# A trunk kernel on one core: the last block's sum and logits move into the first routing, its norm behind its own routing

## Chip, cores and metric

The kernel runs on one core of a Trainium2 chip. The metric is the device time of one execution in microseconds (us). Engines are named as in the profile: PE (products), PEld (PE's weight loads, which overlap them), DVE (vector), ACT (scalar), POOL (GpSimd), SP (which here only issues DMAs).

## What is computed

One layer over 16 learned meta tokens and 512 tokens of width 1024: an input norm, a mixer (stick-breaking attention and an RWKV-7 time mix with gates, then `w_out`), a residual norm, a mixture of experts, a last norm. The last half matters here:

```python
h = layer_norm(ALPHA * h + mix, ln1_g[l], ln1_b[l])
ff = moe_ffn(h, router_w, router_b, wg, wu, wd)
h = layer_norm(ALPHA * h + ff, ln2_g[l], ln2_b[l])
...
logits = (t @ router_w) + router_b          # 16 experts in 4 groups of 4
probs = softmax(logits)
group_score = sum(top_k(grouped, 2)[0])     # best group by its two best experts
gate = top_val / sum(top_val)               # the two best experts of that group
out = sum over experts e of combine[:, e] * ((silu(t @ wg[e]) * (t @ wu[e])) @ wd[e])
```

## The kernel before, in words

The tokens lie in four blocks of 128 (blocks 0 to 3; tiles `hb[0]` to `hb[3]`, printed as hb_5422 to hb_5425). The mixer's end, the routing and the experts follow each other, with every engine's instructions in the order in which the program records them (`in_order`, called after the experts, binds each engine to that order).

*w_out and the residual norm.* For each block b the products of `w_out` (L1319) fill two halves of 512 columns. `half_in(b, n, pt)` adds a half to the scaled residual (L1457) and takes its statistics (L1460); `stats(b)` joins them (L1464, L1466) and has POOL raise the variance to the power -0.5 (L1467). `turn(b, q)` transposes four 128-column pieces on PE (L1475), ACT copies them out (L109, tile h1T). `logits(b, q)` multiplies four pieces with the router's weights (L1484, 16 columns wide); with q = 1 DVE scales the result (L1486, tile lg). `store_h1(b, n)` norms `hb[b]` in place on DVE (L1494 and L1495; for block 3 in two halves) and SP stores it (L1496) into h1_d, from which the experts' tokens are gathered later. The products for block b carry the transposes and logits of block b-1 between them.

*Routing.* `route(lo, hi)` is a generator for blocks lo to hi-1. Its first part (L1385 to L1392, with one ACT exponential) ranks the experts within their groups; then it makes the masks of the chosen experts and expert pairs (L1393 to L1408, tiles msk). Up to the first `yield` all this is one piece. The second piece counts positions: PE products of the pair masks with triangular or full ones (L1413, 24 columns wide), read by DVE (L1415, tile posx). `early = route(0, 3)` does blocks 0 to 2, `late = route(3, 4)` block 3.

*One-hots and picks.* `one_hot_f` turns positions into one-hots (L1514, tile ohf). `pick(b)` multiplies block b with its one-hots (L1509): 8 products of 128 columns, each with two weight loads in the trace, so 16 rows of PEld. Their sums over the four blocks are the tokens of the first tile of expert work, copied out by ACT to the tile x. pick(b) reads `hb[b]` after the norm. The last pick, `pick(3)`, stands outside the shown function, before `gates()`, which computes the gate values on DVE and POOL (L1434 to L1449, tile info).

*Fillers.* `warm(n)` issues n products of the identity with itself (L430), whose result nobody reads. Here 8 stand before the positions of block 3 and 12 behind its one-hot.

*Experts.* 12 tiles of 128 places (4 slots of 32), 6 passes of 16 products each per tile (L1720 for gate and up, L1731 for down), 72 passes in all. 96 weight blocks of 1 MB are fetched by SP (L1293) in the order of use into 18 buffers. A pass that was the last to use a buffer frees it for the next fetch. Between the passes stand the products that make token indices and gates from the one-hots (L1594), POOL's gathers of tokens by index from h1_d (L1623), their transposes (L1639), and the last norm with the scattered store (L1629).

The order around the change is that of the recorded calls:

```python
    logits(3, 0)
    next(early)
    turn(3, 1)
    one_hot_f(0, 3)
    store_h1(3, 1)
    pick(0)
    logits(3, 1)
    late = route(3, 4)
    next(late)
    pick(1)
    pick(2)
    warm(WARM_R[0])
    next(late)
    one_hot_f(3, 4)
    warm(WARM_R[1])
```

Of the kernel before, what the change touches and what calls it, by code (L numbers as in the profile page):

```python
# [44 lines left out]
SOLVE_RATE = 1.0  # L45
SY = (5.0, 1.4, 1.4)
WARM = 16
WARM_R = (8, 12)
HSD = 4
OVT = 6  # L50
LY = 6
# [17 lines left out]
def trunk(ctx, tc, A, out):  # L69
# [29 lines left out]
    def sm():  # L99
        return bank("sm")  # L100
# [7 lines left out]
    def act(out, in_, func, **kw):  # L108
        ins = nc.scalar.activation(out, in_, func, **kw)  # L109
        if func in (AF.Exp, AF.Ln, AF.Sigmoid, AF.Tanh, AF.Silu) and not tc.in_control_flow:  # L110
            if tables["load"] is not None:
                order(ins, tables["load"])
            tables["users"].append(ins)
        return ins
# [310 lines left out]
    def warm(n):  # L425

        if n:
            pw = sm()
            for _ in range(n):
                nc.tensor.matmul(pw[:, 0:128], ident, ident, start=True, stop=True)  # L430
# [931 lines left out]
    def route(lo, hi):  # L1362
# [27 lines left out]
        act(e, e, AF.Exp)  # L1390
        V.tensor_tensor(gt, gt, eq, op=OP.add)
        V.tensor_reduce(rv, gt, axis=AX.X, op=OP.add)  # L1392
        V.scalar_tensor_tensor(tp, rank, 2.0, e, op0=OP.is_lt, op1=OP.mult)  # L1393
        V.tensor_scalar(two, rank, 2.0, None, op0=OP.is_lt)
        V.tensor_reduce(g1.rearrange("p n g -> p (n g)"), tv, axis=AX.X, op=OP.add)
# [74 lines left out]
    def turn(b, q):  # L1470
        if not q:
            TT[b, "T"] = P4.tile([128, KD, 128], FT, name="h1T", bufs=2)
        pt = sm()
        for k in range(4):
            nc.tensor.transpose(pt[:, k * 128:(k + 1) * 128], hb[b][:, (4 * q + k) * 128:(4 * q + k + 1) * 128], ident)  # L1475
        act(TT[b, "T"][:, 4 * q:4 * q + 4], pt.rearrange("p (k t) -> p k t", k=4), AF.Copy)

    def logits(b, q):

        if not q:  # L1480
            TT[b, "l"] = sm()
        pl = TT[b, "l"]
        for k in range(4 * q, 4 * q + 4):
            nc.tensor.matmul(pl[:, 0:NE], TT[b, "T"][:, k, :], rwg[:, k, :], start=k == 0, stop=k == KD - 1)  # L1484
        if q:
            nc.vector.scalar_tensor_tensor(lg[:, b], pl[:, 0:NE], TT[b, "n"][0], rb2, op0=OP.mult, op1=OP.add)  # L1486

    def store_h1(b, n):

        rs, mean = TT[b, "n"]  # L1490
        for h in range(0, 2, n):
            cs = slice(512 * h, 512 * h + 512 * n)
            z = hb[b][:, cs]
            nc.vector.scalar_tensor_tensor(z, z, mean, g1r[:, cs], op0=OP.subtract, op1=OP.mult)  # L1494
            nc.vector.scalar_tensor_tensor(z, z, rs, b1r[:, cs], op0=OP.mult, op1=OP.add)  # L1495
            nc.sync.dma_start(h1_d[128 * b:128 * b + 128, cs], z)  # L1496
# [7 lines left out]
    def pick(b, hs=(1, 0)):  # L1504


        for h in hs:
            for k in range(4):
                nc.tensor.matmul(PX[h][:, k], hb[b][:, 512 * h + 128 * k:512 * h + 128 * k + 128], OHF[:, b],  # L1509
                                 start=b == 0 and k == 0, stop=b == 3 and k == 3)  # L1510

    def one_hot_f(lo, hi):

        nc.vector.tensor_tensor(OHF[:, lo:hi].rearrange("p n (q s) -> p n q s", q=4),  # L1514
                                iota_1[:, None, None, 0:CAP].to_broadcast([128, hi - lo, 4, CAP]),
                                posx[:, lo:hi, 0:4, None].to_broadcast([128, hi - lo, 4, CAP]), op=OP.is_equal)
# [7 lines left out]
    for b in range(4):  # L1524
        pt = acc() if b else PZ[4]
        for k in range(0 if b else 4, 8):
            if k == 2 and b:
                turn(b - 1, 1)
                store_h1(b - 1, 2)
            if k == 3 and b:  # L1530
                logits(b - 1, 0)
            if k == 4 and b:
                logits(b - 1, 1)
            if k == 6:
                turn(b, 0)
            w_out(pt, b, WO[2 + k // 4], k)
            if k == 4 and b == 3:
                PX = [acc().rearrange("p (k t) -> p k t", k=4) for _ in range(2)]
                for u in PX:
                    nc.vector.memset(u, 0.0)  # L1540
                early = route(0, 3)
                next(early)
        half_in(b, 1, pt)
        stats(b)
    logits(3, 0)
    next(early)
    turn(3, 1)
    one_hot_f(0, 3)
    store_h1(3, 1)
    pick(0)  # L1550
    logits(3, 1)
    late = route(3, 4)
    next(late)
    pick(1)
    pick(2)
    warm(WARM_R[0])
    next(late)
    one_hot_f(3, 4)
    warm(WARM_R[1])
    p4.__exit__(None, None, None)  # L1560
    hp_pool.__exit__(None, None, None)

# [381 lines left out]
```

## Time and profile before

| | |
|---|---|
| median of 3 runs | 875.85 us (873.61 to 877.27) |
| the profiled execution | 873.92 us |
| its span, first to last instruction | 872.2 us |
| mean granted TensorE clock | 0.959 |
| PE / PEld busy | 804.0 us (92%) / 522.4 us (60%) |
| DVE / ACT / POOL busy | 422.0 / 317.2 / 294.2 us |
| HBM traffic | 195 GB/s over the span |

The span is what the profiler saw between the first and the last instruction; the execution's time has 1.7 us around it. Times in the rows below count from the start of the span. A row of the timeline gives start, duration, engine, line, operation and tiles (out<-in); a bracket tells how long the engine was idle before it and what ended that. The granted clock (PEclk) is the share of full speed: 1.00 is 2.4 GHz, 0.50 is 1.2 GHz.

### The profile page before, as it was taken

What the parts mean: (1) busy time and instruction counts of PE and PEld (TensorE: products, weight loads), DVE (VectorE), ACT (ScalarE), POOL (GpSimd) and SP (SyncE); (2) the same over time, 40 slices, a digit from 0 to 9 for tenths busy, and PEclk for the clock granted to TensorE, in tenths of its full rate; (3) what the DMA queues carried; (4) which work ended last, traced back from release to release, by engine and by line L of the source; (5) the groups of instructions that cost most, each with busy time, mean ns of one, the idle gap of its engine ahead of it and who ended that gap; (6) DMA issues with size and microseconds to landing.
All of it is one profiled execution on the core that took longest, in us unless ns stands there. A gap on an engine that the chain in (4) does not pass through costs nothing. (4 is left out here: it accounts for less than half of the span.)

```text
span 872.2 us, 16061 instructions
## 1 busy us (share of the span) xinstructions
PE 804.0 (92%) x6476; PEld 522.4 (60%) x6476; DVE 422.0 (48%) x795; ACT 317.2 (36%) x639; POOL 294.2 (34%) x339
## 2 busy tenths in 40 slices
PE   6989999989898989969998999899999999999993
PEld 5877777867888867747666877773333333333331
DVE  7565664741476669981554788720123112202214
ACT  6466564655756575525555332111010010010000
POOL 3266766651433444955552001120101200300102
PEclk8999898999999999988998999889999999999996
DMA  4521111136432225433315979599799999999800
GB/s 149 183 60 49 49 49 50 49 101 222 137 105 86 84 75 157 145 98 98 93 56 174 311 247 390 206 353 325 258 383 387 375 385 387 377 386 386 303 1 27
DMA packets 127234, 169.17 MB, mean 194 GB/s; under 512 B 7106, under 2 KB 62476, under 8 KB 127156
## 3 DMA queue, kind: packets, MB, share of 16 engines
q1 hardware_dynamic: 122228, 158.00, 52.8%
q10 hardware_dynamic: 2944, 5.90, 1.9%
q0 software_dynamic: 1984, 4.21, 1.4%
q8 instruction: 52, 0.85, 0.4%
q14 instruction: 26, 0.21, 0.1%
HBM read 152.29 MB, written 17.89 MB: 195 GB/s over the span
## 5 line engine op out<-in xcount | busy, mean ns | idle before, releaser
L237 POOL TENSOR_TENSOR w_lo<-w_raw,w_hi 128x512 fp32r<-128x512 f32 x87 | 123.4, 1421 | 169.1 <-ACT w_hi L109 151.2
L1720 PE MATMUL bank<-raw,x 128*32 128x512 f32 x1536 | 170.9, 594 | 1.9 <-ACT hid L109 1.2
L335 PE MATMUL bank<-hT_hi,w_hi 128*128 128x264 f32 (+1 forms) x512 | 149.1, 347 | 3.4 <-ACT w_hi L109 1.6
L335 PE MATMUL bank<-hT_hi,w_lo 128*128 128x264 f32 (+1 forms) x512 | 138.6, 327 | 8.0 <-POOL w_lo L237 8.0
L335 PE MATMUL bank<-hT_lo,w_hi 128*128 128x264 f32 (+1 forms) x512 | 137.2, 324 | 0.0
L1720 PEld LDWEIGHTS bank<-raw,x 128*32 128x32 f32 x1536 | 47.9, 110 | 104.8 <-issue 102.3
L335 PEld LDWEIGHTS bank<-hT_hi,w_hi 128*128 128x128 f32 x512 | 87.1, 193 | 18.3 <-ACT w_hi L109 2.7
L335 PEld LDWEIGHTS bank<-hT_hi,w_lo 128*128 128x128 f32 x512 | 86.8, 193 | 16.5 <-POOL w_lo L237 11.6
L335 PEld LDWEIGHTS bank<-hT_lo,w_hi 128*128 128x128 f32 x512 | 86.5, 192 | 7.2
L1731 PE MATMUL bank<-raw,h 128*32 128x512 f32 x768 | 87.0, 594 | 0.0
L1694 POOL TENSOR_TENSOR ln_f<-ln_f,mhalf 128x1 f32<-128x1 f32 x12 | 11.5, 956 | 184.6 <-DVE ln_f L1693 184.6
L109 ACT ACTIVATE w_hi<-w_raw 128x512 fp32r<-128x512 f32 x100 | 62.3, 624 | 24.6 <-DMA w_raw<-in_w_in_dram 9.0
L1649 DVE SCALAR_TENSOR_TENSOR hid<-hid,gat,bank 128x512 f32<-128x512 f32 x12 | 9.0, 747 | 120.9 <-PE bank L1720 64.5
L1731 PEld LDWEIGHTS bank<-raw,h 128*32 128x32 f32 x768 | 23.4, 110 | 50.8 <-issue 50.8
L568 POOL TENSOR_TENSOR R<-zs,R 128x144 f32<-128x144 f32 (+3 forms) x32 | 44.8, 1421 | 18.6 <-DVE R L566 18.6
L1319 PE MATMUL bank<-raw,hT_hi 128*128 128x512 f32 x128 | 44.6, 404 | 0.4 <-ACT hT_hi L109 0.4
L109 ACT ACTIVATE h<-bank 128x512 f32<-128x512 f32 x12 | 7.2, 597 | 97.5 <-PE bank L1639 97.5
L109 ACT ACTIVATE x<-bank 128x512 f32<-128x512 f32 x14 | 8.4, 597 | 83.2 <-PE bank L1639 74.3
L109 ACT ACTIVATE hid<-bank 128x512 f32<-128x512 f32 x12 | 7.1, 595 | 72.3 <-PE bank L1720 72.3
L1467 POOL TENSOR_TENSOR ln_rs<-ln_ve,mhalf 128x1 f32<-128x1 f32 x4 | 5.3, 1328 | 79.2 <-DVE ln_ve L1466 79.2
L566 DVE TENSOR_TENSOR_SCAN R<-ones_r,ab 128x144 f32<-128x144 f32 (+3 forms) x32 | 31.9, 1036 | 0.0
L556 DVE COPY zs<-bank 128x264 f32<-128x264 f32 (+3 forms) x40 | 15.3, 432 | 33.9 <-ACT ab L109 33.8
(349 smaller groups left out, 1334.5 us busy)
## 6 DMA issues: line engine op xcount, KB each, us to landing
raw<-in_exp_w_gate_dram SPq DMA_DIRECT2D x32, 1024.0 KB
raw<-in_exp_w_up_dram SPq DMA_DIRECT2D x32, 1024.0 KB
raw<-in_exp_w_down_dram SPq DMA_DIRECT2D x32, 1024.0 KB
w_raw<-in_w_in_dram SPq DMA_DIRECT2D x84, 256.0 KB
raw<-in_w_out_dram SPq DMA_DIRECT2D x4, 1024.0 KB
sig_d<-sg ACTq DMA_DIRECT2D x8, 264.0 KB
sig<-sig_d SPq DMA_DIRECT2D x8, 264.0 KB
xin<-in_x_dram SPq DMA_DIRECT2D x4, 512.0 KB
```

What stands on the lines that cost most here:

```text
L109: ins = nc.scalar.activation(out, in_, func, **kw)
L237: eng.tensor_tensor(lo[:, ks], raw[:, ks], hi[:, ks].bitcast(FT), op=OP.subtract)
L335: nc.tensor.matmul(pt[:, :e - s], w_[:, k % 4, :], m[:, k, s:e], start=(k == 0 and n == 0), stop=(k == KD - 1 and n == 2))
L556: nc.vector.tensor_copy(zs[:, h, s:e], pz[h][:, :e - s])
L566: nc.vector.tensor_tensor_scan(R[:, h, :W][:, ::-1], ones_r[:, :W], ab[:, h, :W][:, ::-1], 0.0, op0=OP.mult, op1=OP.add)
L568: nc.gpsimd.tensor_tensor(R[:, h, :W], z[:, h], R[:, h, :W], op=OP.subtract)
L1319: nc.tensor.matmul(pt, MG[x][:, k, 128 * b:128 * b + 128], w[y][:, k % 4, :], start=(k == 0 and i == 0), stop=(k == 7 and i == 2))
L1467: nc.gpsimd.tensor_tensor(rs, ve, mhalf, op=OP.pow)
L1649: nc.vector.scalar_tensor_tensor(hid, hid, gate, pu, op0=OP.mult, op1=OP.mult)
L1694: nc.gpsimd.tensor_tensor(rs, ve, mhalf, op=OP.pow)
L1720: nc.tensor.matmul(P[k[0]][32 * i:32 * i + 32], x_of(t, i, kk), W[k, e][0][:, s], start=kk == 0, stop=kk == 7)
L1731: nc.tensor.matmul(Y[g, p // 2][r:r + 32], H[t][:, s, 32 * i:32 * i + 32], W[unit_of(k, i), e][0][:, s], start=s == 0 and not second, stop ...
```

## The change

The routing's generator gets one more `yield`, between the ranks and the masks. The last block's sum (`half_in(3, 1)` and `stats(3)`) is recorded after the ranks of blocks 0 to 2 and before their masks. The second half of its logits goes ahead of the positions of blocks 0 to 2 and of all picks; its ranks and masks are taken directly behind the first one-hots; its norm and store go behind its own one-hot, in front of pick(2) and pick(3). Of twenty fillers four are left, ahead of pick(0).

```diff
-WARM_R = (8, 12)
+WARM_R = 4
...
         V.tensor_tensor(gt, gt, eq, op=OP.add)
         V.tensor_reduce(rv, gt, axis=AX.X, op=OP.add)
+        yield
         V.scalar_tensor_tensor(tp, rank, 2.0, e, op0=OP.is_lt, op1=OP.mult)
...
     logits(3, 0)
     next(early)
     turn(3, 1)
+    logits(3, 1)
+    next(early)
     one_hot_f(0, 3)
-    store_h1(3, 1)
-    pick(0)
-    logits(3, 1)
+    warm(WARM_R)
     late = route(3, 4)
     next(late)
+    next(late)
+    pick(0)
     pick(1)
-    pick(2)
-    warm(WARM_R[0])
     next(late)
     one_hot_f(3, 4)
-    warm(WARM_R[1])
+    store_h1(3, 1)
+    pick(2)
```

The lines of the changed kernel are one higher from the new `yield` on (L1415 becomes L1416) and two higher behind this stretch (L1594 becomes L1596). How the instructions stand on the two engines concerned:

PE before, from the end of the positions of blocks 0 to 2 (tile msk_2213) to the first expert products (raw: weights):

```order
L1413 MATMUL bank<-msk_2213,tri 128x24
L1475 MATMUL bank<-ident,hb_5425 128x128 x4
L1509 MATMUL bank<-ohf,hb_5422 128x128 x8
L1484 MATMUL bank<-rwg,h1T 128x16 x4
L1509 MATMUL bank<-ohf,hb_5423 128x128 x8
L1509 MATMUL bank<-ohf,hb_5424 128x128 x8
L430 MATMUL bank<-ident 128x128 x8
L1413 LDWEIGHTS ones_b
...
L430 MATMUL bank<-ident 128x128 x12
L1509 MATMUL bank<-ohf,hb_5425 128x128 x8
L1720 MATMUL bank<-raw,x 32x512 x16
```

PE now, from the first half of block 3's logits on:

```order
L1485 MATMUL bank<-rwg,h1T 128x16 x4
L1476 MATMUL bank<-ident,hb_5425 128x128 x4
L1485 MATMUL bank<-rwg,h1T 128x16 x4
L1414 LDWEIGHTS tri
...
L430 MATMUL bank<-ident 128x128 x4
L1510 MATMUL bank<-ohf,hb_5422 128x128 x8
L1510 MATMUL bank<-ohf,hb_5423 128x128 x8
L1414 LDWEIGHTS ones_b
...
L1510 MATMUL bank<-ohf,hb_5424 128x128 x8
L1510 MATMUL bank<-ohf,hb_5425 128x128 x8
L1722 MATMUL bank<-raw,x 32x512 x16
```

The transposes and the second logits of block 3 went ahead of the first positions; the positions of block 3 went ahead of pick(2); between picks 0 and 1 nothing is left, and pick(3) follows pick(2) directly.

DVE now, from the ranks of blocks 0 to 2 to the ranks of block 3 (before, the four rows from hb_5425 to ln_ve stood behind the pair masks, and the scaled logits lg behind the norm of block 3):

```order
L1392 TENSOR_REDUCE r_rank<-r_gt 128x48
L1458 SCALAR_TENSOR_TENSOR hb_5425<-hb_5425,bank 128x512
L1461 BN_STATS l_st<-hb_5425 128x6
L1465 BN_AGGR ln_mv<-l_st 128x2
L1467 TENSOR_SCALAR ln_ve<-ln_mv 128x1
L1394 SCALAR_TENSOR_TENSOR r_tp<-r_rank,r_e 128x48
...
L1409 TENSOR_TENSOR msk_2213<-msk_2212 128x24
L1487 SCALAR_TENSOR_TENSOR lg<-bank,ln_rs,rb_2219 128x16
L1416 SCALAR_TENSOR_TENSOR posx<-bank,msk_2213 128x72
L1515 TENSOR_TENSOR ohf<-iota_2191,posx 128x384
L1385 TENSOR_TENSOR r_eq<-lg 128x64
```

And DVE now, behind the positions of block 3 (before, r_ky of the gates came directly behind the one-hot):

```order
L1416 SCALAR_TENSOR_TENSOR posx<-bank,msk_2213 128x24
L1515 TENSOR_TENSOR ohf<-iota_2191,posx 128x128
L1495 SCALAR_TENSOR_TENSOR hb_5425<-hb_5425,ln_mv,g1r 128x512
L1496 SCALAR_TENSOR_TENSOR hb_5425<-hb_5425,ln_rs,b1r 128x512
L1495 SCALAR_TENSOR_TENSOR hb_5425<-hb_5425,ln_mv,g1r 128x512
L1496 SCALAR_TENSOR_TENSOR hb_5425<-hb_5425,ln_rs,b1r 128x512
L1435 TENSOR_TENSOR r_ky<-e_2200,msk_2212 128x64
```

The four norm steps of block 3 stand between its one-hot and the gates. ACT and POOL keep their order; on SP the read of the overflow flag (tile xc_i) goes from the middle of the expert loads to behind the last one, and the two stores of block 3 keep their place ahead of the loads that follow them.

## Rows read from the trace of the kernel before

**Rows 1.** Table of stretches: busy (count) of PE, PEld, DVE, ACT, POOL; PEclk, DMA share, GB/s.

```profile
600.00:860.00 260.00, 256.97 (x2416) 83.15 (x2408) 52.44 (x130) 19.27 (x33) 31.59 (x29) 1.00 0.87 316
820.00:840.00 20.00, 20.00 (x188) 6.17 (x184) 0.75 (x1) 1.19 (x2) 0.00 (x0) 1.00 0.20 75
```

**Rows 2.** Timeline, PE and PEld, from w_out's end to the experts.

```profile
557.99 0.40 PE L1319 MATMUL bank<-raw,hT_hi 128*128 128x512 f32 x1
...
558.29 1.06 PE L1484 MATMUL bank<-rwg,h1T 128*128 128x16 f32 x8
...
560.59 0.19 PE L1413 MATMUL bank<-msk,tri 128*128 128x24 bf16 x1 [1.24 <-DVE msk L1408]
...
561.17 0.66 PE L1475 MATMUL bank<-ident,hb 128*128 128x128 f32 x4 [0.27 <-DVE hb L1457]
...
563.06 3.49 PEld L1509 LDWEIGHTS bank<-ohf,hb 128*128 128x128 f32 x16 [1.47 <-DVE ohf L1514]
...
566.42 1.83 PEld L1484 LDWEIGHTS bank<-rwg,h1T 128*128 128x128 f32 x8
...
573.57 1.87 PEld L430 LDWEIGHTS bank<-ident 128*128 128x128 f32 x16
...
575.36 0.24 PEld L1413 LDWEIGHTS <-ones_b 128*128 128x128 bf16 x3
...
578.22 1.87 PEld L1509 LDWEIGHTS bank<-ohf,hb 128*128 128x128 f32 x16
...
580.97 3.64 PE L1720 MATMUL bank<-raw,x 128*32 128x512 f32 x32 [0.69 <-ACT x L109]
```

**Rows 3.** Table of stretches, as rows 1: the picks.

```profile
562.00:572.00 10.00, 8.94 (x42) 8.94 (x43) 6.50 (x25) 1.96 (x3) 2.71 (x6) 0.50 0.57 194
572.00:581.00 9.00, 8.31 (x80) 8.11 (x80) 2.42 (x10) 1.20 (x2) 2.21 (x7) 1.00 1.05 390
```

**Rows 4.** Timeline, DVE, the same stretch.

```profile
558.25 0.21 DVE L1393 SCALAR_TENSOR_TENSOR r_tp<-r_rank,r_e 128x48 f32<-128x48 f32 x1
...
560.43 0.68 DVE L1457 SCALAR_TENSOR_TENSOR hb<-hb,bank 128x512 f32<-128x512 f32 x1
...
562.19 0.22 DVE L1415 SCALAR_TENSOR_TENSOR posx<-bank,msk 128x72 f32<-128x72 f32 x1
562.45 0.56 DVE L1514 TENSOR_TENSOR ohf<-iota,posx 128x384 f32<-128x384 f32 x1
562.92 0.74 DVE L1494 SCALAR_TENSOR_TENSOR hb<-hb,ln_mv,g1r 128x512 f32<-128x512 f32 x1
...
565.26 0.75 DVE L1495 SCALAR_TENSOR_TENSOR hb<-hb,ln_rs,b1r 128x512 f32<-128x512 f32 x1
...
568.67 0.23 DVE L1385 TENSOR_TENSOR r_eq<-lg 128x64 f32<-128x64 f32 x1
...
571.29 0.17 DVE L1408 TENSOR_TENSOR msk<-msk 128x8 bf16<-128x8 bf16 x1
575.76 0.18 DVE L1415 SCALAR_TENSOR_TENSOR posx<-bank,msk 128x24 f32<-128x24 f32 x1 [4.31 <-PE bank L1413]
...
576.19 0.22 DVE L1434 TENSOR_TENSOR r_ky<-e,msk 128x64 f32<-128x64 f32 x1
```

**Rows 5.** Timeline, ACT: the copy behind block 3's last transposes.

```profile
561.86 0.60 ACT L109 ACTIVATE h1T<-bank 128x512 f32<-128x512 f32 x1 [3.62 <-PE bank L1475]
```

**Rows 6.** Timeline, SP's queue: the first expert load behind the stores.

```profile
566.46 0.39 SPq L1293 DMA_DIRECT2D raw<-in_exp_w_up_dram  x1
```

**Rows 7.** Timeline, POOL and PEld: gates' end, first gather, its first use.

```profile
579.97 0.21 POOL L1449 TENSOR_TENSOR info<-r_ab,info 128x8 bf16<-128x8 f32 x1
586.44 1.20 POOL L1623 DMA_INDIRECT hb<-h_d,idx  x1 [6.26 <-DMA g2h<-in_ln_g_dram]
...
592.73 0.42 PEld L1639 LDWEIGHTS bank<-ident,hb 128*128 128x128 f32 x4 [0.84 <-DMA hb<-h_d,idx]
```

**Rows 8.** Table of stretches, as rows 1: an earlier slow stretch.

```profile
384.00:398.00 14.00, 10.24 (x158) 7.54 (x160) 6.29 (x6) 4.73 (x8) 6.90 (x7) 0.51 0.25 75
```

## The prediction

> **What bounds the kernel now.** Start at the end. The table of stretches for 600 to 860 us shows PE busy 256.97 of 260 us at a clock of 1.00 [rows 1]: the expert stage is one unbroken row of products, so whatever moves its first product (L1720) moves the end by as much. The table also shows the cover of that claim: the DMA engines are busy only 0.20 of 820 to 840 us, some 4 us of full traffic, so the last weights are in near 824, while products go on to about 857 (260 less 257 us is 3 us of idle time at the end) [rows 1]. Next, the timeline says what the first expert product waits for. It starts at 580.97, released by ACT's copy of the gathered tokens, which is released by the last product of `pick(3)` [rows 2]. So read PE backwards from there: pick(3) 578.22, the position products of block 3 (L1413) at 575.36, fillers (L430) from 573.57, picks 1 and 2 before them, the second half of the logits of block 3 from 566.42 for 1.83, pick(0) from 563.06 [rows 2]. The clock of this stretch is 0.50 from 562 to 572 and 1.00 after it [rows 3]. That is 1.2 and 2.4 GHz, and the same 16 weight loads take 3.36 us (563.06 to 566.42) at the one and 1.79 us (573.57 to 575.36) at the other [rows 2].
>
> On DVE the masks of block 3 are done at 571.29 + 0.17 = 571.46 [rows 4], yet their products start at 575.36: they stand behind picks 1 and 2 and eight fillers. The twelve further fillers then hold pick(3) until 578.22, though its one-hot is finished by about 576.2, when the next DVE operation (r_ky) begins [rows 2, 4].
>
> **The change, step by step.** I call X the moment when the position products of block 3 start on PE (575.36 before; the expert stage follows 580.97 - 575.36 = 5.61 later).
>
> *Sum of block 3 ahead.* Its four DVE steps now follow the rank instead of the masks. They can start when the last w_out product ends, 557.99 + 0.40 = 558.4 [rows 2]. From the sum to the operation behind the variance took 562.19 - 560.43 = 1.76 [rows 4], so the second half of the first routing starts at 560.2 instead of 558.25. From it to the mask products took 560.59 - 558.25 = 2.34 [rows 2, 4], so those come at 562.6, 2.0 later than before. This is the cost of the move.
>
> *Logits of block 3 early.* The transposes came 561.17 - 560.43 = 0.74 behind the start of the sum [rows 2, 4]: now 559.2, directly behind the first half of the logits (558.29 + 1.06 = 559.35). The copy starts 0.69 behind them and takes 0.60 [rows 5], so the second half of the logits runs from 560.5 to 561.6, in a hole in which PE only waits for masks. It leaves the middle of the picks, where it took 1.83 us at half clock [rows 2]. POOL's power for the scale is issued at the same distance behind the variance as before and is wanted two microseconds later: free.
>
> *First pick.* The positions are read 0.40 behind the start of their products (575.36 to 575.76), the one-hot follows 0.26 later (562.19 to 562.45) and pick(0) 0.61 after that (562.45 to 563.06) [rows 2, 4]: 562.6 + 0.4 + 0.26 + 0.61 = 563.8. The four fillers in front are eight loads: 0.9 us at full and 1.7 us at half rate behind mask products that end near 562.75, so 563.7 or 564.5. I take 564.5, 1.4 later than before.
>
> *Masks of block 3.* They begin 0.47 behind the start of the one-hot (562.45 to 562.92), at 563.7, and take 571.29 - 568.67 = 2.62 [rows 4]: ready near 566.5, long before PE gets to them. So X is now set by PE alone: pick(0) and pick(1), 32 loads, no logits and no fillers between.
>
> *How long that takes is the unknown*, since it is the clock's. Lower end: 32 loads at 1.79 / 16 = 0.112 is 3.6 us, from 563.8: X = 567.4. Upper end: all at 3.36 / 16 = 0.21 is 6.8 us, from 564.5: X = 571.3. Before, PE waited 1.24 us for the masks, 0.27 for the sum and 1.47 for the one-hot among narrow products, and the clock fell [rows 2, 3]. The changed order still has a wait of some 0.7 us for the copy and 1.0 us for the masks among products 16 and 24 columns wide, so I expect the fall again, after these waits. It came back about 9 us after pick(0) began, with the narrow logits in between; behind these, picks alone ran for 572 - 568.2 = 3.8 us until it rose. Without the logits I take some 4 us of half rate from 564.5: 4.1 / 0.213 = 19 loads, the other 13 at 0.112 in 1.5 us, X = 570.1.
>
> *Norm of block 3 behind its routing.* It now stands between the one-hot and pick(3), which reads the normed block. From X: positions 0.40, then one-hot and next operation 0.43 (575.76 to 576.19), then four norm steps that took 565.26 + 0.75 - 562.92 = 3.09 [rows 4], the left half done after some 1.5 of them. The left half is ready at X + 2.4, the right at X + 3.9. On PE, pick(2) covers X + 0.2 to X + 2.0, half of pick(3) X + 2.4 to X + 3.3, the other half X + 3.9 to X + 4.8. The copy and its release took 580.97 - 578.22 - 1.79 = 0.96 behind the last load [rows 2]. The experts start at X + 5.75: PE waits about 1.0 us for DVE here, which it did not before.
>
> *Result of the chain.* X = 570.1 gives 575.8, 5.2 us before 580.97; the ends 567.4 and 571.3 give 573.1 (7.8 earlier) and 577.0 (3.9 earlier).
>
> *What moves behind it.* SP: the two stores of block 3 stood ahead of seven expert loads, the first issued at 566.46 [rows 6]; the stores now wait for the norm (X + 3.9 = 574.0), so the loads go about 8 us later. Cover: the program first wants one of them in the eighth pass of products, 7 passes of about 3.6 us (the first is 3.64 [rows 2]) or 25 us after the start. Lag and earlier start together are 8 + 5.2 = 13 us, less than the 33 us from the last weights to the last product, even if half of those are the last passes' own; if that cover were gone, what exceeds it would come back as a stall. SP's read of the overflow flag moves behind its last load and holds nothing. DVE and POOL: the gates start at X + 3.9; from r_ky to the end of POOL's last step took 579.97 + 0.21 - 576.19 = 4.0 [rows 4, 7], so they are done at X + 7.9, and are wanted after the first pass, X + 5.75 + 3.6 = X + 9.3. Spare 1.4 us, was 4.4. POOL: the first token gather is issued at 586.44, 5.5 us behind the first product, and used by the transposes at 592.73 [rows 7]; this shifts as a whole, but the delayed loads now stand in the DMA queues beside it. Bounds 0 and 2.7 us (one more block of 1 MB at the 390 GB/s of 572 to 581 [rows 3]); I take 0.2, near the lower, since the engines were already full then (share 1.05).
>
> Sum: 5.2 - 0.2 = 5.0 us. The profiled execution took 873.92 us, 872.2 of it span; so 868.9 for one like it. It lies 1.9 below the median of 875.85; against the median, 870.8.
>
> **The clock rule.** The trace shows the clock down for 10 us in a stretch where PE was busy 8.94 of 10.00 us [rows 3]. The Trainium skill ("TensorE: Matmul & The Clock Gate", Part 1, "What's actually happening") says that "the default state is throttled, and activity releases the throttle". It speaks against taking away sixteen of the twenty fillers, whose only output is activity; by it alone the low clock could last through all picks, which is the third rival below. The trace agrees so far that a stretch of narrow products does not keep the clock up.
>
> **Rivals.** 0.5% of 875.85 is 4.4 us, about what a measurement here can tell from no change.
>
> 1. *The clock never falls*, or only for a moment: X = 567.4, 7.8 - 0.2 = 7.6 us, 868.2. For it: the waits among the narrow products shrink from 1.24 + 0.27 + 1.47 us to about 1.9 us, with fillers before pick(0). Against: what PE does between them is still narrow. Chance 0.12.
> 2. *Low through both first picks, or a late gather*: X = 571.3, 3.9 less 0 to 2.7; about 872.4. Chance 0.20.
> 3. *Low to the last pick*: 48 loads at 0.213 = 10.2 us and 0.2 from 564.5 end at 574.9, pick(3) at 578.3, experts at 579.3: 1.7 earlier, 874.2. For it: the fillers are gone and PE now waits for the norm as well; from 384 to 398 us the clock was 0.51 with PE busy 10.24 of 14.00 us [rows 8]. Against: unbroken picks brought it back in 3.8 us. Chance 0.13.
> 4. *Low into the experts, slower than before.* If the waits for the norm keep or bring the low clock at the first expert products, each pass of 3.6 us becomes about 7.2 at half rate. After rival 3 (1.7 gained) one such pass loses 1.9 net, and from the second on it shows: 7.2 - 1.7 = 5.5 us, 881.4. Against: the waits are 0.4 and 0.6 us within 3 us of full-width products, and the 0.69 us wait before the experts left the clock at 1.00 [rows 2, 3]. Chance 0.05.
>
> That the change doesn't do what it says is partly so already: pick(2) is meant to cover the norm and covers half of it; that is in the sum.
>
> **How the numbers follow.** The forecast (X between 569.5 and 571.0, 869.9 to 871.8) has chance 0.50 and is the likeliest: 870.8. Its upper edge crosses 4.4 us of gain: I count 0.46 of it as faster. Faster: 0.46 + 0.12 = 0.58. Same: 0.04 + 0.20 + 0.13 = 0.37. Slower: 0.05. The range takes in the forecast, rival 1 (868.2) and rival 2 with half of the gather's bound, 0.82 together, and half a microsecond of scatter at the ends: 867.6 to 873.6.
>
> **What would show it.** In the changed profile: transposes of block 3 near 559.2 and the logits ahead of the mask products near 562.6; pick(0) between 563.7 and 564.6; X near 570 with nothing between the picks before it; PE waiting about 0.4 and 0.6 us for hb from L1496 inside pick(3); experts 5.75 behind X and from there 291 us to the end. It is wrong if the clock is 0.50 at the first expert pass, if PE waits for DVE or POOL at L1596, for the gather at L1641, or for a weight.

## Result and the profile after

The changed kernel takes 870.09 us in the median of six runs (869.74 to 872.0). The kernel before, run beside it, took 877.74 us (873.61 to 879.67). The ratio on record is 0.9935 with a 95% interval of 0.9906 to 0.9964 (it is not the quotient of these two medians, which is 0.9913). So it is faster, as forecast, though the upper end of the interval falls short of the 0.5% that the prediction counted as faster. The forecast was 870.8, in a range of 867.6 to 873.6. One run in this document, of the kernel before without fillers (882.11 us), was in a slower state and is left out of its median and ratio. The profiled execution took 870.13 us with a span of 868.4, against 873.92 and 872.2 before.

Spans of two profiles can't be subtracted as they are. The last `w_out` product starts at 557.99 before [rows 2] and at 559.76 now, and in the twelve other profiles of this study at 557.93 to 565.15, although nothing that PE does ahead of it was edited. So I count from that start, written with a plus sign: experts at +22.98 means 22.98 us behind it.

Timeline of PE in the changed kernel, from that product to the first use of gathered tokens (columns as in [rows 2]; L1485 logits, L1414 positions, L430 fillers, L1510 picks, L1722 experts):

```profile
559.76 0.40 PE L1319 MATMUL bank<-raw,hT_hi 128*128 128x512 f32 x1
...
562.29 1.06 PE L1485 MATMUL bank<-rwg,h1T 128*128 128x16 f32 x8 [0.69 <-ACT h1T L109]
564.46 0.18 PE L1414 MATMUL bank<-msk,tri 128*128 128x24 bf16 x1 [1.10 <-DVE msk L1409]
...
564.62 2.05 PE L430 MATMUL bank<-ident 128*128 128x128 f32 x8
566.46 4.34 PE L1510 MATMUL bank<-ohf,hb 128*128 128x128 f32 x32
570.63 0.23 PE L1414 MATMUL bank<-msk,ones_b 128*128 128x24 bf16 x3
...
572.95 1.16 PE L1510 MATMUL bank<-ohf,hb 128*128 128x128 f32 x8 [0.18 <-DVE hb L1496]
574.40 1.16 PE L1510 MATMUL bank<-ohf,hb 128*128 128x128 f32 x8 [0.29 <-DVE hb L1496]
576.24 3.64 PE L1722 MATMUL bank<-raw,x 128*32 128x512 f32 x32 [0.69 <-ACT x L109]
...
589.25 0.66 PE L1641 MATMUL bank<-ident,hb 128*128 128x128 f32 x4 [1.17 <-DMA hb<-h_d,idx]
```

The positions of block 3 now stand directly behind picks 0 and 1. The experts start at +16.48 (576.24 - 559.76) instead of +22.98, which is 6.50 earlier. Two new waits follow the edit: pick(3) waits twice for the norm (hb, L1496), and the transposes of the first gathered tokens wait 1.17 us for a DMA.

The stretches of the same profile (columns as in [rows 1]):

```profile
560.00:570.00 10.00, 8.21 (x62) 7.84 (x62) 7.22 (x36) 2.10 (x4) 2.13 (x6) 0.83 0.01 2
564.30:567.71 3.41, 3.25 (x20) 3.25 (x20) 2.85 (x17) 1.46 (x2) 0.00 (x0) 0.50 0.02 5
...
581.70:589.20 7.50, 6.38 (x76) 1.90 (x68) 0.17 (x1) 0.00 (x0) 3.22 (x3) 1.00 1.05 334
...
600.00:855.00 255.00, 252.98 (x2386) 81.17 (x2374) 51.04 (x124) 18.77 (x33) 31.52 (x29) 1.00 0.91 335
815.00:835.00 20.00, 20.00 (x192) 6.13 (x188) 0.75 (x1) 1.19 (x2) 0.00 (x0) 1.00 0.35 130
```

The clock of 0.50 is there for 3.41 us only; before, it held from 561.80 to 572.04. The expert stage is the unbroken row it was [rows 1], and the later expert loads are still in before the end (DMA share 0.35 from 815 to 835 us, with products to about 854; 0.20 at the like place before). No product of the expert stage waits for a weight.

While the first gather is under way, from 581.70 to 589.20, the DMA engines are full (share 1.05).

DVE's timeline of the stretch that [rows 4] shows of before: the masks of block 3 end, DVE waits for PE, reads the positions, makes the one-hot (left out) and norms block 3 (the last of four steps shown):

```profile
568.16 0.16 DVE L1409 TENSOR_TENSOR msk<-msk 128x8 bf16<-128x8 bf16 x1
570.93 0.18 DVE L1416 SCALAR_TENSOR_TENSOR posx<-bank,msk 128x24 f32<-128x24 f32 x1 [2.61 <-PE bank L1414]
...
573.59 0.75 DVE L1496 SCALAR_TENSOR_TENSOR hb<-hb,ln_rs,b1r 128x512 f32<-128x512 f32 x1
```

The late masks no longer set anything (DVE waits 2.61 us behind them), but the norm's last step ends at 574.34, and the second half of pick(3) starts with it.

The books close as follows. The experts start 6.50 earlier. From there to the end takes 292.16 us (868.4 - 576.24) instead of 291.23 (872.2 - 580.97), 0.93 more. So 5.57 us are gained, and 1.77 of them are hidden in the two spans by the later start of the counting point: 5.57 - 1.77 = 3.8 = 872.2 - 868.4.

### The profile page after: what moved, and what is told of

The parts are those of the page before. It is cut to its first block, busy times and chain, and to the rows that moved or that the text cites. A ratio compares the mean times of both kernels' runs of the same rounds, so it can differ in the third digit from the quotient of the medians.

```text
span 868.4 us, 15998 instructions
## 1 busy us (share of the span) xinstructions
PE 797.8 (92%) x6444; PEld 518.9 (60%) x6444; DVE 423.8 (49%) x795; ACT 317.5 (37%) x639; POOL 290.4 (33%) x339
## 5 line engine op out<-in xcount | busy, mean ns | idle before, releaser
L237 POOL TENSOR_TENSOR w_lo<-w_raw,w_hi 128x512 fp32r<-128x512 f32 x87 | 115.8, 1332 | 170.4 <-ACT w_hi L109 151.5
L1722 PE MATMUL bank<-raw,x 128*32 128x512 f32 x1536 | 170.8, 594 | 1.9 <-ACT hid L109 1.2
L1722 PEld LDWEIGHTS bank<-raw,x 128*32 128x32 f32 x1536 | 47.7, 110 | 105.0 <-issue 101.8
```

What stands on the lines that cost most here:

```text
L237: eng.tensor_tensor(lo[:, ks], raw[:, ks], hi[:, ks].bitcast(FT), op=OP.subtract)
L1722: nc.tensor.matmul(P[k[0]][32 * i:32 * i + 32], x_of(t, i, kk), W[k, e][0][:, s], start=kk == 0, stop=kk == 7)
```

## The experiments

All runs in one table, in us. "Low" is how long the clock was 0.50 behind the last `w_out` product, "positions" the PE start of block 3's, "experts" the first expert product, "rest" from there to the end, "gather" PE's wait for the first gathered tokens. Ratios are against the kernel before, on the same chip; the medians of two rows can come from two chips.

| kernel | low | positions | experts | rest | gather | median, ratio [95%] |
|---|---|---|---|---|---|---|
| before | 10.24 | +17.48 | +22.98 | 291.23 | 0 | |
| changed | 3.41 | +10.87 | +16.48 | 292.16 | 1.17 | 870.09, 0.9935 [0.9906, 0.9964] |
| changed, again | 3.41 | +10.87 | +16.47 | 292.12 | 1.18 | 869.07, 0.9916 [0.9875, 0.9958] |
| before without fillers | 10.24 | +15.39 | +18.99 | 291.93 | 0.90 | 874.53, 0.9978 [0.9936, 1.002] |
| changed with before's fillers | 3.41 | +12.38 | +19.67 | 291.41 | 0.32 | 873.95, 0.9992 [0.9954, 1.003] |
| waits filled | 0 | +9.58 | +15.19 | 291.36 | 0.40 | 869.39, 0.9948 [0.9917, 0.9978] |
| no fillers | 6.83 | +12.05 | +17.66 | 292.39 | 1.15 | 873.81, 0.9956 [0.9918, 0.9994] |
| no fillers, again | 6.83 | +12.13 | +17.74 | 292.12 | 1.11 | 869.76, one run |
| norm early | 3.41 | +10.86 | +16.05 | 291.98 | 1.00 | 872.15, 0.9949 [0.9921, 0.9976] |
| loads early | 6.83 | +12.16 | +17.77 | 292.30 | 1.34 | 871.16, 0.9947 [0.9923, 0.9970] |
| row loads late | 3.41 | +10.78 | +16.38 | 292.30 | 1.07 | 871.79, 0.9953 [0.9921, 0.9984] |
| indices early | 3.41 | +10.81 | +16.42 | 290.19 | 0 | 870.87, 0.9917 [0.9885, 0.9949] |
| waits filled, indices early | 0 | +9.60 | +15.20 | 290.18 | 0 | 866.77, 0.9878 [0.9839, 0.9917] |
| the same, norm split | 0 | +9.58 | +14.19 | 290.23 | 0 | 868.29, 0.9908 [0.9873, 0.9944] |

Runs of one kernel lie up to 11 us apart (870.79 to 881.65 for the kernel before, on one chip), so the timed ratios tell effects of some 3 us and more, and the profiles, at the place of the edit, tell tenths.

### Fillers and order apart

The kernel before, its twenty fillers gone:

```diff
-WARM_R = (8, 12)
+WARM_R = (0, 0)
```

> The kernel before in its own order, without its twenty fillers. All times are counted from the start of the last w_out product (557.99 before, 559.76 in the changed kernel); there the experts start at +22.98 before and at +16.48 changed. Theory A (the fillers are plain work on the path, and the clock does without them): the positions of block 3 start when pick(2) ends, 573.57, instead of 575.36; pick(3) follows 1.27 later (0.66 to the one-hot, 0.61 from there to the pick), takes 1.79, and the copy 0.96, so the experts start 4.0 behind the positions instead of 5.61: 577.6, that is +19.6, 3.4 us earlier than before, and the time falls by 3.4. Theory B (the fillers buy the clock): without them the clock of 0.50 goes on through pick(3) and its 16 loads take 3.36 instead of 1.79, experts at +21.2, 1.8 us gained; if it goes on into the first pass, that pass takes some 7.2 us instead of 3.6 and the run is 1.8 us slower than before. Theory C (order alone matters, the fillers only fill waits): experts at +23.0, no change.

The changed kernel, with the fillers of before put back:

```diff
     pick(1)
+    warm(8)
     next(late)
     one_hot_f(3, 4)
     store_h1(3, 1)
     pick(2)
+    warm(12)
```

> The changed kernel with the fillers of before put back: 8 ahead of the positions of block 3 and 12 ahead of pick(3), beside the 4 that it has. Counted from the last w_out product, the changed kernel has these positions at +10.76 and the experts at +16.48. Theory A (fillers are plain work on the path): 16 loads at 0.112 put the positions 1.8 later, +12.6; the other 24 loads run behind pick(2), from 2.0 to 4.7 behind the positions, where the norm of block 3 would have held pick(3) until 3.9 anyway; pick(3) then runs unbroken to 6.5, and the experts start 7.5 behind the positions, +20.0: 3.5 us later than in the changed kernel and 3.0 earlier than before. Theory B (fillers buy the clock): the stretch at 0.50 is shorter than 3.4 us and the positions come at +11.5 or earlier. Theory C (fillers only fill waits, the order is all of the gain): experts at +16.5 to +17.0.

Timeline of PE, before without fillers (L1413 positions, L1509 picks, L1720 experts):

```profile
561.88 0.40 PE L1319 MATMUL bank<-raw,hT_hi 128*128 128x512 f32 x1
...
572.10 5.33 PE L1509 MATMUL bank<-ohf,hb 128*128 128x128 f32 x32
577.27 0.23 PE L1413 MATMUL bank<-msk,ones_b 128*128 128x24 bf16 x3
...
578.13 2.05 PE L1509 MATMUL bank<-ohf,hb 128*128 128x128 f32 x16 [0.61 <-DVE ohf L1514]
580.87 3.64 PE L1720 MATMUL bank<-raw,x 128*32 128x512 f32 x32 [0.69 <-ACT x L109]
```

And the changed order with the fillers of before:

```profile
560.92 0.40 PE L1319 MATMUL bank<-raw,hT_hi 128*128 128x512 f32 x1
...
571.51 1.95 PE L430 MATMUL bank<-ident 128*128 128x128 f32 x16
573.30 0.23 PE L1414 MATMUL bank<-msk,ones_b 128*128 128x24 bf16 x3
...
575.27 2.84 PE L430 MATMUL bank<-ident 128*128 128x128 f32 x24
...
580.59 3.64 PE L1724 MATMUL bank<-raw,x 128*32 128x512 f32 x32 [0.69 <-ACT x L109]
```

Theory A holds in both. The missing fillers alone bring the experts 3.99 us forward (+22.98 to +18.99; 3.4 expected), the order alone 3.31 (to +19.67; 3.0 expected), both together 6.50. The two parts add up to 7.30, which is 0.80 more. Of that, 0.22 lies behind the positions: from there to the experts the missing fillers save 1.90 in the order of before (5.50 to 3.60) and 1.68 in the changed one (7.29 to 5.61), where part of the twelve runs while pick(3) would wait for the norm anyway. The other 0.58 lies ahead of the positions, which the missing fillers move by 2.09 in the one order and 1.51 in the other. There the clock differed too: the low stretch began and ended 0.64 earlier without the fillers than in the kernel before, and 0.47 earlier with the order alone than in the changed kernel, so more of the picks ran at full clock. Some 0.3 of the 3.99 (2.09 less the 1.79 that eight fillers take [rows 2]) is therefore not the fillers' own. Without any filler the clock was low for 10.24 us, as long as with them. So the fillers of before bought nothing there: the first of them stood at 573.57, behind the end of the low stretch at 572.04. The times agree with the traces but prove little alone, since both intervals include no change.

### The clock between the picks

The changed kernel once more, unaltered:

> The changed kernel once more, unaltered, for a second look at the clock. In its first profile the granted clock was 0.50 for 3.41 us (564.30 to 567.71). The run with early expert loads, whose products stand in the same order on PE, had 6.83 us of it. Theory A (the length of the low stretch is chance between two or more lengths for one and the same order): this run shows 3.4, 6.8 or 0 us, the positions of block 3 at +10.8, +12.2 or +9.5 behind the last w_out product and the experts at +16.5, +17.8 or +15.2. Theory B (the early loads lengthened it, and the order alone gives 3.41): 3.4 us again, experts at +16.5 within 0.1. The wait for the first token gather: 1.0 to 1.4 us.

It shows 3.41 us and +16.47 again.

Fillers in PE's two waits ahead of the picks:

```diff
     turn(3, 1)
+    warm(3)
     logits(3, 1)
+    warm(5)
     next(early)
```

> The changed kernel with eight fillers more: three between the transposes of block 3 and the second half of its logits, where PE waits 0.69 us for the copy, and five behind these logits, where it waits 1.10 us for the masks. Theory A (PE's waits in the narrow stretch bring the low clock, 564.30 to 567.71 in the changed kernel): with the waits filled the clock stays at 1.00 or is low for less, the positions of block 3 come at +8.5 to +9.5 behind the last w_out product instead of +10.76, and the experts 1.2 to 2.2 us earlier than +16.48. Theory B (the narrow products themselves, with 16 and 24 columns, are what counts, or the clock falls anyway): the stretch at 0.50 stays near 3.4 us and the positions at +10.8, the experts at +16.5. Theory C: fillers run past the waits at half rate and delay what they stand before, experts at +16.9 or later.

Stretch and PE timeline with the waits filled:

```profile
560.00:570.00 10.00, 9.98 (x93) 9.60 (x94) 7.61 (x39) 2.10 (x3) 2.15 (x6) 1.00 0.01 2
```

```profile
561.23 0.83 PE L430 MATMUL bank<-ident 128*128 128x128 f32 x6
...
562.99 1.36 PE L430 MATMUL bank<-ident 128*128 128x128 f32 x10
...
565.46 3.84 PE L1510 MATMUL bank<-ohf,hb 128*128 128x128 f32 x32
569.13 0.23 PE L1414 MATMUL bank<-msk,ones_b 128*128 128x24 bf16 x3
```

PE is busy 9.98 of 10.00 us instead of 8.21, and the granted clock stays at 1.00. The 32 loads of picks 0 and 1 end 1.29 earlier and the experts start at +15.19: Theory A. The same held in both later versions that keep these fillers. The Trainium skill ("TensorE: Matmul & The Clock Gate", Part 1, "What's actually happening") has activity release the throttle; the trace agrees, for work in two waits of 0.69 and 1.10 us. Whether the closed waits or the full-width products in them did it, this run does not tell apart.

The four fillers of the change taken away:

```diff
-WARM_R = 4
+WARM_R = 0
```

> The changed kernel without its last four fillers. In its profile the eight weight loads of these took 1.78 us at half rate and pick(0) started 0.4 behind the end of its one-hot. Theory A (they are plain work): pick(0) starts at 564.46 + 0.40 + 0.26 + 0.61 = 565.73 instead of 566.25, 0.5 earlier, and with the clock as before the experts at +16.0. Theory B (they shorten the low stretch): the clock is at 0.50 for longer than 3.41 us, and the positions come 0.8 us or more later, experts at +17.3 or later.

> The changed kernel without its four fillers, a second look. In its first profile the clock was low for 6.82 us and the experts came at +17.66, where the changed kernel showed 3.41 us and +16.48 twice. Theory A (the missing fillers lengthen the low stretch): 6.8 us again or longer, experts at +17.3 to +17.9. Theory B (chance, as in the run with early loads, which has the four fillers and showed 6.83 us): any of 3.4 and 6.8; with 3.4 the experts come at +16.0 to +16.3.

Timeline of PE, the second of these runs:

```profile
564.07 6.36 PE L1510 MATMUL bank<-ohf,hb 128*128 128x128 f32 x32 [0.92 <-DVE ohf L1515]
...
575.88 3.64 PE L1722 MATMUL bank<-raw,x 128*32 128x512 f32 x32 [0.69 <-ACT x L109]
```

The low stretch was 6.83 us in both, and the experts came at +17.66 and +17.74: 1.2 us lost where plain work would have gained 0.5. Six profiles with the four fillers and without filled waits or early loads show 3.41 us. The two runs without fillers have the clock fall at +4.41 and +4.42; the run with early indices (below), with the four fillers, has it fall at +4.41 too (568.10 - 563.69), and low for half as long. So by these profiles the four fillers earn more than they cost.

It is not a law, though: the run with early loads (below) has PE's rows in the order of the changed kernel, fillers included, and showed 6.83 us. There the clock fell at +3.81 (561.74 - 557.93), earlier than in the six (+4.07 to +4.54); whether that made the stretch longer, and what moved it, wasn't isolated. The two low stretches, early indices first (columns as in [rows 1]):

```profile
568.10:571.51 3.41, 3.13 (x20) 3.13 (x20) 2.87 (x17) 1.34 (x2) 0.00 (x0) 0.50 0.02 5
561.74:568.57 6.83, 5.93 (x33) 5.93 (x33) 4.10 (x24) 1.50 (x2) 0.86 (x2) 0.50 1.03 383
```

### The norm's new place

The norm of block 3 back ahead of its ranks:

```diff
     one_hot_f(0, 3)
+    store_h1(3, 1)
     warm(WARM_R)
...
     one_hot_f(3, 4)
-    store_h1(3, 1)
     pick(2)
```

> The changed kernel with the norm of block 3 back ahead of its ranks, directly behind the first one-hots, so that this one part of the change is undone. Theory A (the norm's new place gains nothing: it frees the masks of block 3 by as much as pick(3) then waits for it): DVE's four norm steps take 3.05 us, so the masks of block 3 end 3.05 later than at 568.32, +11.6 behind the last w_out product, and their products start at +11.7 instead of +10.76, PE waiting 0.9 us for them; pick(3) then waits for nothing and the experts start 4.8 behind these products instead of 5.72: +16.5, the same as in the changed kernel for a low stretch of 3.41 us. Theory B (the new place is worth what it frees on DVE): experts at +17.5 or later. SP's expert loads start some 5 us earlier; PE's wait for the first gather stays at 0.9 us or more if it doesn't come from those loads, and falls below 0.4 if it does.

Timeline of PE:

```profile
559.27 0.40 PE L1319 MATMUL bank<-raw,hT_hi 128*128 128x512 f32 x1
...
570.13 0.23 PE L1414 MATMUL bank<-msk,ones_b 128*128 128x24 bf16 x3
570.79 0.17 PE L1414 MATMUL bank<-msk,tri 128*128 128x24 bf16 x1 [0.44 <-DVE msk L1409]
570.82 3.82 PE L1510 MATMUL bank<-ohf,hb 128*128 128x128 f32 x32
575.32 3.64 PE L1722 MATMUL bank<-raw,x 128*32 128x512 f32 x32 [0.69 <-ACT x L109]
```

PE waits 0.44 us for the masks (0.9 expected), then picks 2 and 3 run as one block. The experts start at +16.05 (+16.5 expected), 0.43 earlier than in the changed kernel: pick(2) starts 0.57 later, but from there to the experts it takes 4.50 us instead of 5.50. So this part of the change gains nothing on the path and loses a little, by the waits of [0.18] and [0.29] and by what pick(3) does in halves. The gain by order is that of the sum, the logits and the masks together.

### The wait for the first gather

Four expert loads issued ahead of block 3's logits:

```diff
+    for n in range(11, 15):
+        fetch()
     logits(3, 0)
```

> The changed kernel with four expert loads recorded ahead of the first half of block 3's logits, so that SP issues them before the stores of block 3. Theory A (PE's wait of 1.17 us for the first token gather comes from the expert loads that the change made late, which now run beside it): the loads run before the picks, when the DMA engines are little used; the wait at the transposes of the gathered tokens is 0.3 us or less, and from the experts' start to the end of the span it takes 291.0 us instead of 292.16. The experts' start stays at +16.48 behind the last w_out product, within 0.2. Theory B (the gather waits for POOL or for the store of the norm, which also came late): the wait stays at 0.9 us or more and the time does not move. Theory C (loads beside the stores of blocks 0 to 2 delay something that the routing needs): experts later than +16.8.

The rows of the last norm loaded later by ACT:

```diff
-        if n == 1:
+        if n == 8:
             g2h, b2h = half_bc(A["ln2_g"], "g2h"), half_bc(A["ln2_b"], "b2h")
```

> The changed kernel with ACT's loads of the last norm's two rows (g2h and b2h, four loads of 128 KB) issued behind the ninth pass of products instead of the second. In the changed kernel ACT issues them from 575.60 to 578.56, 3 to 6 us ahead of the first gather at 581.72, while the expert loads fill the DMA engines. Theory A (the gather stands behind these half-megabyte of row loads, and that is the wait of 1.17 us): without them in front the wait is 0.4 us or less, and from the experts' start to the end of the span it takes 291.4 us or less instead of 292.16. Theory B (the expert loads in flight alone set how long a gather takes): the wait stays at 0.9 us or more, 292.0 or more. The experts' start is not touched: +16.5 for a low stretch of 3.41 us, +17.7 for one of 6.83.

Both remedies failed: the waits are 1.34 and 1.07 us. With the norm early, where SP's loads go out early too, it is 1.00:

```profile
568.49 0.39 SPq L1293 DMA_DIRECT2D raw<-in_exp_w_up_dram  x1
```

In the changed kernel that row stands at 574.78. So the row loads do not make this wait. The expert loads are not cleared, since neither the run with early loads nor the one with the norm early had them through when the gather was issued. An estimate of what was left then takes the stores and loads that SP had issued, less what its queue (q1) had moved: 0.8 MB in the kernel before (two stores and seven loads, 7.86 less 7.03), 3.7 in the changed kernel (two and five, 5.77 less 2.09), 2.6 with early loads (four of them issued from 574.21 on) and 2.8 with the norm early. The queue's rows (packets, MB, share of the engines), from 564.00 to 586.44 before and from 573.00 to 581.72 in the changed kernel:

```profile
q1 hardware_dynamic: 3557, 7.03, 87.7%
q1 hardware_dynamic: 1068, 2.09, 74.3%
```

The gather's own queue (q0) in the 4.00 us behind the issue, in the kernel before:

```profile
q0 software_dynamic: 62, 0.16, 10.9%
```

In none of the other thirteen profiles did it move a packet in that time, and there 2.4 to 4.5 MB were left. So the transfers left at the issue may be the cause. That is not shown: no run changed them alone, and among the thirteen the delay doesn't grow with them.

The indices made ahead of the first expert pass:

```diff
+    sl = slots(0)
+    next(sl)
+    next(sl)
     gates()
     while free:
         fetch()
-    sl = slots(0)
-    next(sl)
     next(sl)
+    for i in (1, 2, 0):
+        get_x(0, i)
     for n, (k, t) in enumerate(passes):
...
-            next(sl)
-            for i in (1, 2, 0):
-                get_x(0, i)
```

> The changed kernel with the one-hots of the places ahead of the gate values on DVE, the products for the first token indices between pick(3) and the first expert pass instead of behind that pass, and the three gathers behind them. PE waits 0.69 us for ACT there, and 24 of these products took about 0.5. Theory A (PE's wait of 1.17 us comes from when the gather is issued: it is used 6.7 to 7.7 us after its issue wherever PE waited for it, and PE reaches the transposes 6.3 us after it): the gather is issued near 578.2 instead of 581.72 and landed before PE wants it, the wait is gone, experts at +16.5 within 0.2 for the same clock, and from their start to the end 290.5 us, the wait of 1.17 and the 0.5 of the products less than 292.16. Theory B (the gather waits for the store of the norm, or is served only when the expert loads in flight allow it, whenever it is issued): it is issued 3.5 us earlier but used less than 1 us earlier, and a wait of 0.5 us or more stays. Theory C: the one-hots are late on DVE and hold the first expert pass, experts at +17 or later.

POOL's first gather, its issue in the changed kernel:

```profile
581.72 1.20 POOL L1625 DMA_INDIRECT hb<-h_d,idx  x1 [3.47 <-DVE idx L1603]
```

and with early indices, with PE's rows around it (L1596 the products for indices, then the first two expert passes):

```profile
583.48 1.20 POOL L1625 DMA_INDIRECT hb<-h_d,idx  x1 [0.87 <-issue]
```

```profile
563.69 0.40 PE L1319 MATMUL bank<-raw,hT_hi 128*128 128x512 f32 x1
...
579.36 0.57 PE L1596 MATMUL bank<-info,oh 128*64 128x2 bf16 x24
580.11 7.07 PE L1722 MATMUL bank<-raw,x 128*32 128x512 f32 x64 [0.19 <-ACT x L109]
...
591.24 0.66 PE L1641 MATMUL bank<-ident,hb 128*128 128x128 f32 x4
```

The gather is issued 3.37 behind the first expert product instead of 5.48, and the transposes have no wait before them. The products for the indices fill 0.5 of the 0.69 us in which PE waited for ACT. From the experts' start to the end it takes 290.19 us (870.3 - 580.11; 290.5 expected) instead of 292.16. Theory A holds as to the remedy, though the issue came 2.1 us earlier and not the 3.5 expected. PE wants the tokens 6.3 us behind the issue in both kernels (592.73 - 586.44 = 6.29 before [rows 7], 589.25 - 1.17 - 581.72 = 6.36 now), and in the ten profiles in which it had to wait they came 6.68 to 7.70 us behind it. In the kernel before, the bracket of PEld's row puts its last 0.84 us of idle time down to the gather [rows 7], so it landed between 5.45 and 6.29 us behind its issue: less than 0.84 us to spare. With early indices PEld's row has the same bracket, 7.76 us behind the issue, so little is to spare there too. Why the gather was quicker before is as open as the cause of the wait.

### Versions that beat both

Both remedies, filled waits and early indices, in one kernel:

> The changed kernel with both: eight more fillers in PE's two waits, as in the run that filled them, and the first token indices ahead of the first expert pass. Theory A for both parts: no clock of 0.50 from 555 to 600 us, experts at +15.2 within 0.2 behind the last w_out product, no wait for the first gather, and from the experts' start to the end 290.5: 2.9 us less than the changed kernel by its first profile (1.3 for the start, 1.6 behind it). Theory B (the clock's rise was chance): a stretch at 0.50 of 3 us or more in spite of the fillers, experts at +16.5 or later.

It gives what the two gave apart: no low clock, experts at +15.20, and 290.18 us from there. The time is 866.77 us, 0.9878 [0.9839, 0.9917].

Then the norm cut in two, its left half into DVE's wait ahead of the positions (the third argument of `store_h1` now names the halves to do):

```diff
     pick(1)
+    store_h1(3, 1, (0,))
     next(late)
     one_hot_f(3, 4)
-    store_h1(3, 1)
+    store_h1(3, 1, (1,))
     pick(2)
```

> The version with filled waits and early token indices, and with the norm of block 3 cut in two: its left half stands behind the masks of block 3 and ahead of the positions, where DVE waited 1.33 us for PE, its right half behind the one-hot as before. Theory A (pick(3) waits for DVE as the prediction counted, 0.4 and 0.6 us): the left half takes 1.5 us and ends 0.2 after DVE would have read the positions, so the one-hot comes 0.2 later and the right half is done 1.3 earlier; pick(3) follows pick(2) without a wait, and the experts start at +14.4 to +14.6 behind the last w_out product instead of +15.20. From there to the end 290.2 as before. Theory B (PE's waits there only move to the copy of x or to the one-hot): +15.0 or later.

Timeline of DVE, then of PE:

```profile
568.33 0.83 DVE L1495 SCALAR_TENSOR_TENSOR hb<-hb,ln_mv,g1r 128x512 f32<-128x512 f32 x1
569.20 0.75 DVE L1496 SCALAR_TENSOR_TENSOR hb<-hb,ln_rs,b1r 128x512 f32<-128x512 f32 x1
569.86 0.18 DVE L1416 SCALAR_TENSOR_TENSOR posx<-bank,msk 128x24 f32<-128x24 f32 x1
```

```profile
559.88 0.40 PE L1319 MATMUL bank<-raw,hT_hi 128*128 128x512 f32 x1
...
569.57 3.82 PE L1510 MATMUL bank<-ohf,hb 128*128 128x128 f32 x32
573.31 0.57 PE L1599 MATMUL bank<-info,oh 128*64 128x2 bf16 x24
574.07 7.07 PE L1725 MATMUL bank<-raw,x 128*32 128x512 f32 x64 [0.19 <-ACT x L109]
```

Picks 2 and 3 run in one block of 32 without a wait, and the experts start at +14.19, 1.01 earlier still (0.6 to 0.8 expected). By the trace this is the shortest: 304.42 us from the last `w_out` product to the end (864.3 - 559.88), against 305.38 for the version before it, 308.64 for the changed kernel and 314.21 before. By the runs the last two versions can't be told apart (0.9908 [0.9873, 0.9944] against 0.9878), and both intervals overlap with those of the changed kernel (0.9935 and 0.9916): that they are ahead of it, too, rests on the traces.

## Why the prediction was right, and where it was off

The gain came where the prediction put it, and nearly all of its steps can be read off [rows 2] and the rows above. The sum came out in part by luck, as two of its terms were off in opposite directions.

- **The cost of the move** was 2 us. The second half of the logits was forecast at 560.5, that is +2.5, and came at +2.53 (562.29). The mask products were forecast at +4.6 and came at +4.70, pick(0) at +6.5 and its loads came at +6.49.
- **X is set by PE alone.** The masks of block 3 were forecast ready at +8.5 and are at +8.56; DVE then waits 2.61 us for PE. Right.
- **Half-rate time is the term that was mis-sized.** The step "some 4 us of half rate from 564.5: 19 loads" failed twice over. The stretch was 3.41 us long, and it began at +4.54, before the four fillers, so it was over at +7.95 while picks had run for 1.5 us. The 32 loads took 4.35 us; with 0.213 and 0.112 us a load that is (4.35 - 32 x 0.112) / 0.101 = 7.6 of them at half rate, not 19. This brings X to +10.76 (first weight load, 570.52) where +12.1 was forecast.
- **The norm** behaved as counted: two waits for hb (0.37 and 0.48 us by PE's weight loads, 0.4 and 0.6 forecast), and experts 5.72 behind X against 5.75. That its new place gains nothing was not in the prediction; the run with the norm early shows it.
- **The gather** cost 0.93 net, with a wait of 1.17, where 0.2 was taken of a range of 0 to 2.7. The step took 0.2 because the DMA engines were already full before. They were, with a share of 1.05 during the first gather in both kernels, but by the estimate above 0.8 MB of SP's transfers were left at its issue before and 3.7 now. Whether the delayed loads, which the step gave as the reason to fear for it, made the wait stays open. What the prediction did not price is that [rows 7] give little margin for this gather: it was wanted 6.29 us behind its issue and had landed less than 0.84 earlier, and in every profile in which PE waited for it, it took 6.7 to 7.7.
- **Covers that held:** no wait for the gates, none for a weight, clock 1.00 from the first expert product on.

The two errors have opposite signs: 1.3 us better at the experts' start, 0.7 worse behind it. The forecast was 5.0 us of gain; the trace has 5.57. That the medians differ by more, 7.65 us, can't be given to the change beyond this: the interval of the ratio is 3.2 to 8.3 us, and the scatter ahead of the edit alone is several us. The forecast was counted from a median of 875.85 for the kernel before, which beside the changed one measured 877.74; that the time forecast and the one measured agree to 0.7 us is luck within this scatter.

Of the rivals, the first (the clock never falls) is what the kernel with filled waits does, and its X there is close to the 567.4 forecast: +9.47 by its first weight load (569.02) against +9.4. The late gather of the second happened without the rest of it. The third and fourth did not occur in any profile.

## What to carry to other kernels

In this kernel fillers held a path in one place and bought clock in another: fill the waits ahead of the narrow products, where the clock is lost, and put none between finished inputs and the product that waits for them. When a stage is moved forward, price the transfers that were just in time before: the row that used them without a wait gives only an upper bound on what they need, so look for a way to issue them earlier in the same edit, and count what is left in the queues when they are issued. And compare profiles from a point just ahead of the edit, since the scatter before it can be larger than the effect.

## What the hardware showed

The clock fell to 0.50 in a stretch with PE busy 8.21 of 10.00 us and no wait over 1.10, and eight dummy products in two waits kept it at 1.00 in all three kernels that had them. One and the same order of PE's rows had a low stretch of 3.41 us in three profiles, where the clock fell at +4.47 to +4.54, and, with other loads running beside it and the fall at +3.81, one of 6.83 in a fourth; the difference was 1.29 us at the positions. A token gather issued while the DMA engines were full (share 1.04 to 1.06) took 6.7 to 7.7 us until its first tokens were used, in the ten profiles in which PE waited for it. In the kernel before, with the engines as full but 0.8 MB of SP's transfers left at its issue instead of 2.4 to 4.5, it took at most 6.29. The Trainium skill ("DMA: Bandwidth & Descriptors", "Queues, rings and completion order") says that each engine goes round its queues packet by packet. That would fit the ten, in which the delay doesn't follow what is left in SP's queue, but not the kernel before; no run here settles it.
